# Scores of two heads into one double bank of PSUM, shared with the projections' sums

## The chip, the cores and the metric

The kernel runs on one core of a Trainium2 chip. The metric is device time in microseconds (us) of one execution. The engines are named as in the profile: PE (TensorE, matmuls; PEld its weight loads), DVE (VectorE), ACT (ScalarE), POOL (GpSimd), SP (SyncE, which issues the DMAs). PSUM, which the matmuls write, has eight banks of 512 fp32 numbers in each of 128 partitions; DVE and ACT read their sums from there.

## The reference

A stack of decoder layers on x of 256 positions by 1024, all in fp32: two layers of feed-forward, attention, feed-forward, and then a second block with other mixers and a routed feed-forward. The edit touches the attentions of the two first layers. NSA (16 query heads of 64, 4 key heads) adds a compressed branch, a selected one and a window one under gates; at 256 positions the last two have all keys in reach. DIFF (8 heads) takes the difference of two softmaxes per head:

```python
def dense_diff_attention(q, k, v, slopes, lmbda):
...
        sc = jnp.einsum('bhctd,bhcsd->bhcts', qi, k).astype(f32) * scale \
            - slopes[:, None, None, None] * dist
        p = masked_softmax(sc, dist >= 0)
        a = p[:, :, 0] - lmbda * p[:, :, 1]
        return jnp.einsum('bhts,bhsd->bhtd', a.astype(v.dtype), v)

def nsa_mixer(h, w_in, w_out, q_norm, k_norm, cmp_pos, cmp_w1, cmp_w2):
...
    o_cmp, o_sel = nsa_compressed_selected(q, kc, vc, ks, vs, slopes)
    o_win = banded_attention(q, kw, vw, slopes, NSA_WINDOW)
    g = jax.nn.sigmoid(gates.reshape(B, S, NSA_HKV, G, 3).transpose(0, 2, 3, 1, 4))
    o = g[..., 0:1] * o_cmp + g[..., 1:2] * o_sel + g[..., 2:3] * o_win
    return o.transpose(0, 3, 1, 2, 4).reshape(B, S, NSA_HQ * dh) @ w_out
...
        x = x + 0.5 * swiglu(rmsnorm(x, ffn1_norm[layer]), ffn1_w_in[layer], ffn1_w_out[layer])
...
        x = x + y
        x = x + 0.5 * swiglu(rmsnorm(x, ffn2_norm[layer]), ffn2_w_in[layer], ffn2_w_out[layer])
```

## The kernel before

x stays in SBUF as two tiles of 128 rows. Weights are streamed: SP loads a piece `raw`, ACT rounds it to `whi` (L123), DVE takes the rest `wlo` (L124), and a product with it is three matmuls (L183 to L185: high by high, low by high, high by low; 128x512 each). A projection chunk (`proj_chunk`, L277) sums both row tiles over 1024 inputs: 48 such matmuls into two banks, which `pair` (L194) hands out. `out_proj` (L303) sums the attention's output against its weights into four banks.

NSA runs its parts in an order written out by hand. "a" is an attend of row tile i and key head g, "q" the second query projection, "c" the compressed branch of a tile, "k" its combine, "m" the compression and "o" the output's parts:

```python
NSA_ORDER = "m a00 a01 a10 a11 q c0 a02 a03 o k0 c1 a12 a13 k1"
```

The first query projection, queries(0), stands ahead of all that. A query projection is the chunk, then for each tile an evacuation on ACT (L579), a square (L494), a sum and an inverse root on DVE (L495 on), a product (L581), four transposes on PE (L584) and a copy on ACT (L585). An attend (L664) computes, for each of four heads, a score matmul (L674) whose contraction has 64 rows, rows 0 to 63 for even heads and 64 to 127 for odd ones, and then two softmax parts: DVE adds the bias and takes the minimum in one pass (L504), ACT exponentiates (L507). Probabilities are scaled, transposed (L694), copied (L696, L698) and multiplied by v (L700). The compressed branch's first products are L714, the combine's L747.

DIFF projects six chunks in the order 2, 0, 4, then attends two row tiles of the first four heads, then 1, 3, 5 and the other four heads. An attend (L822) has two scores per head, again on rows 0 to 63 and 64 to 127 (L833), the two softmax parts, the difference, transposes (L843) and the product with v (L846). At the end the output is split and transposed (L233).

Within these lists the order on each engine is worked out by a scheduler when the kernel is built: what stands later in the program can be put between earlier instructions of an engine, where its banks and buffers are free. The banks are dealt out in pools. In NSA: tp two, mm two (projections, compression), sa two (scores), ot one, cm one. In DIFF: tp two, mm two, sa two, pa one, ot one. After the attends all but tp are closed, and the same six banks are dealt again, four of them as mm for `out_proj`.

## Time and profile before

| | us |
|---|---|
| three runs | 2269.57, 2267.53, 2270.04 |
| median | 2269.57 |
| the profiled execution, its own time | 2267.65 |
| its span in the profile | 2265.9 |
| PE busy | 2214.5 |
| DVE busy | 1643.8 |
| ACT busy | 1137.3 |

The span is the stretch from the first to the last recorded instruction of the profiled execution; its own time is 1.75 us longer. Busy times are sums over the records of an engine. A matmul's record is longer than the step from one to the next, since they are pipelined: a row of 0.39 us in a timeline follows the one before it by 0.23. NSA's attention lies between some 225 and 385 us of the span, DIFF's between 750 and 930.

### The profile page before, as it was taken

How to read it: one execution, taken by the hardware profiler on the slowest of the kernel's cores; microseconds unless marked ns; L12 is line 12 of the kernel's file. 1: busy time of each engine (PE TensorE's matmuls, PEld its weight loads, DVE VectorE, ACT ScalarE, POOL GpSimd, SP SyncE). 2: the span in 40 equal slices, each digit the busy share in tenths (PEclk: the TensorE clock that was granted, in tenths of full speed). 3: DMA queues.
4: the chain of work that ended last, by engine and by line, in shares of the span. 5: the costliest groups of instructions: out<-in, count | busy, mean ns of one | idle time of the engine just before them, and what ended most of it. 6: DMA issues, size and time to landing. Idle time of an engine off the chain costs nothing. (4 is left out here: it accounts for less than half of the span.)

```text
span 2265.9 us, 35790 instructions
## 1 busy us (share of the span) xinstructions
PE 2214.5 (98%) x13730; PEld 1875.1 (83%) x13730; DVE 1643.8 (73%) x3303; ACT 1137.3 (50%) x1789; POOL 33.3 (1%) x75
## 2 busy tenths in 40 slices
PE   8999999999999998999999999999999999999999
PEld 7887646888788776888787777999999998888887
DVE  6867666997787587787577567896767767885555
ACT  6554575554555464655455444454533344334443
POOL 1000000000000002000000000000000000000000
PEclk9999989999999997999999999999999999999999
DMA  6654424888655442555432125445544445445554
GB/s 215 195 190 170 154 70 148 298 272 269 237 198 182 166 150 74 163 190 193 130 138 85 66 85 194 140 168 195 184 161 149 150 167 186 159 155 180 195 194 150
DMA packets 107563, 383.33 MB, mean 169 GB/s; under 512 B 13440, under 2 KB 13824, under 8 KB 107392
## 3 DMA queue, kind: packets, MB, share of 16 engines
q1 hardware_dynamic: 103392, 374.39, 48.7%
q10 hardware_dynamic: 3360, 4.55, 0.6%
q8 instruction: 108, 1.77, 0.3%
q0 software_dynamic: 640, 2.11, 0.3%
q14 instruction: 63, 0.52, 0.1%
HBM read 378.89 MB, written 2.11 MB: 168 GB/s over the span
## 5 line engine op out<-in xcount | busy, mean ns | idle before, releaser
L123 ACT ACTIVATE whi<-raw 128x1024 fp32r<-128x1024 f32 x654 | 690.7, 1059 | 767.5 <-PE pout L184 205.0
L124 DVE TENSOR_TENSOR wlo<-raw,whi 128x1024 fp32r<-128x1024 f32 x654 | 797.7, 1223 | 327.1 <-ACT whi L123 318.7
L191 PE MATMUL pair<-xx,whi 128*128 128x512 f32 x1280 | 449.8, 396 | 0.0
L192 PE MATMUL pair<-xx,wlo 128*128 128x256 f32 x1280 | 359.8, 281 | 0.0
L183 PE MATMUL pu<-xx,whi 128*128 128x256 f32 x1024 | 292.6, 286 | 1.1 <-ACT H L1628 1.1
L184 PE MATMUL pu<-xx,wlo 128*128 128x256 f32 x1024 | 290.2, 283 | 0.0
L185 PE MATMUL pu<-xx,whi 128*128 128x256 f32 x1024 | 290.1, 283 | 0.0
L191 PEld LDWEIGHTS pair<-xx,whi 128*128 128x128 f32 x1280 | 240.8, 188 | 55.7 <-issue 0.2
L192 PEld LDWEIGHTS pair<-xx,wlo 128*128 128x128 f32 x1280 | 242.7, 190 | 0.5 <-issue 0.2
L183 PE MATMUL pout<-whi,hs 128*128 128x512 f32 x512 | 201.4, 394 | 0.2 <-ACT hs L1715 0.2
L184 PE MATMUL pout<-whi,hs 128*128 128x512 f32 x512 | 199.5, 390 | 0.2 <-DVE hs L1716 0.2
L185 PE MATMUL pout<-wlo,hs 128*128 128x512 f32 x512 | 199.6, 390 | 0.0
L183 PEld LDWEIGHTS pu<-xx,whi 128*128 128x128 f32 x1024 | 197.0, 192 | 1.3 <-ACT H L1628 1.3
L184 PEld LDWEIGHTS pu<-xx,wlo 128*128 128x128 f32 x1024 | 196.5, 192 | 0.0
L185 PEld LDWEIGHTS pu<-xx,whi 128*128 128x128 f32 x1024 | 196.4, 192 | 0.0
L183 PE MATMUL pair<-whi,hT 128*128 128x512 f32 x352 | 138.5, 393 | 6.6 <-DVE x L350 6.6
L185 PE MATMUL pair<-wlo,hT 128*128 128x512 f32 x352 | 139.2, 396 | 0.0
L184 PE MATMUL pair<-whi,lT 128*128 128x512 f32 x352 | 138.3, 393 | 0.0
L183 PE MATMUL bank<-whi,xx 128*128 128x512 f32 x288 | 118.0, 410 | 1.1 <-DVE rsg L167 0.5
L184 PE MATMUL bank<-whi,xx 128*128 128x512 f32 x288 | 115.7, 402 | 0.0
L185 PE MATMUL bank<-wlo,xx 128*128 128x512 f32 x288 | 114.9, 401 | 0.0
L185 PEld LDWEIGHTS pout<-wlo,hs 128*128 128x128 f32 x512 | 96.1, 188 | 20.2
(562 smaller groups left out, 3505.5 us busy)
## 6 DMA issues: line engine op xcount, KB each, us to landing
raw<-in_pu_dram SPq DMA_DIRECT2D x128, 512.0 KB, 3.5
raw<-in_pv_dram SPq DMA_DIRECT2D x128, 512.0 KB, 3.5
raw<-in_f1i_dram SPq DMA_DIRECT2D x88, 512.0 KB, 4.1
raw<-in_f2i_dram SPq DMA_DIRECT2D x88, 512.0 KB, 4.3
araw<-in_wada_dram SPq DMA_DIRECT2D x48, 512.0 KB, 4.7
raw<-in_f1o_dram SPq DMA_DIRECT2D x44, 512.0 KB, 3.5
raw<-in_f2o_dram SPq DMA_DIRECT2D x44, 512.0 KB, 3.7
raw<-in_wi_dram SPq DMA_DIRECT2D x28, 512.0 KB, 3.4
```

Source lines behind the costliest of these rows:

```text
L123: nc.scalar.activation(hi, raw, AF.Copy)
L124: nc.vector.tensor_tensor(lo, raw, hi.bitcast(F32), op=OP.subtract)
L183: mm(out, lh, rh, start=start, stop=False)
L184: mm(out, ll, rh, start=False, stop=False)
L185: mm(out, lh, rl, start=False, stop=stop)
L191: mm(out, lh, rr, start=start, stop=False)
L192: mm(out[:, 0], ll, rr[:, 0], start=False, stop=stop)
```

## The change

A pool of two double banks ("pairs") takes the place of mm and sa in both attentions. `pair` now hands out one double bank for a projection chunk, the compression takes half of one, and an attend takes one for the scores of two heads (NSA) or of a head's two softmaxes (DIFF). Both score matmuls are written ahead of the softmax parts of either. ot, cm and pa are opened ahead of the pairs. Bank counts stay eight.

```diff
+    def pair_banks(self, ctx, n):
+
+        self.mm = ctx.enter_context(self.tc.tile_pool(name=self.name("pairs"), bufs=n, space=PSUM, reuse_waits="tile"))
+        self.pairs = True
...
-            self.banks(first, mm=2, sa=2, ot=1, cm=1)
+            self.banks(first, ot=1, cm=1)
+            self.pair_banks(first, 2)
...
-                ph = self.bank(self.mm, 256)
+                ph = self.pair()[1][0][:, :256]
...
-                for j in range(4):
-                    h = 4 * g + j
-                    r = slice(64 * (h % 2), 64 * (h % 2) + 64)
-                    ps = self.bank(self.sa, 512)
-                    nc.tensor.matmul(ps[:, :n], qT[r, h // 2, t], KT[r, g, :n], start=True, stop=True)
-                    for b in range(2):
-                        src = ps[:, :n].rearrange("p (k c) -> p k c", c=256)[:, :, b * P:(b + 1) * P]
-                        self.softmax_part(src, self.bias[:, h, 1 - i:], i + 1, sums[:, b, j:j + 1], prob[j][:, b])
+                for j in range(0, 4, 2):
+
+                    ps = self.pair()[1]
+                    for e in range(2):
+                        r = slice(64 * e, 64 * e + 64)
+                        nc.tensor.matmul(ps[e][:, :n], qT[r, 2 * g + j // 2, t], KT[r, g, :n], start=True, stop=True)
+                    for e in range(2):
+                        for b in range(2):
+                            src = ps[e][:, :n].rearrange("p (k c) -> p k c", c=256)[:, :, b * P:(b + 1) * P]
+                            self.softmax_part(src, self.bias[:, 4 * g + j + e, 1 - i:], i + 1, sums[:, b, j + e:j + e + 1],
+                                              prob[j + e][:, b])
...
+            self.pairs = False
             first.close()
             self.banks(ctx, mm=4)
...
-            self.banks(first, mm=2, sa=2, pa=1, ot=1)
+            self.banks(first, pa=1, ot=1)
+            self.pair_banks(first, 2)
...
-                    prob = []
+                    prob, ps = [], self.pair()[1]
                     for e in range(2):
                         r = slice(64 * e, 64 * e + 64)
-                        ps = self.bank(self.sa, 512)
-                        nc.tensor.matmul(ps[:, :n], qT[r, h, t], kT[r, h, :n], start=True, stop=True)
-                        prob.append(self.softmax_part(ps[:, :n].rearrange("p (k c) -> p k c", c=P),
+                        nc.tensor.matmul(ps[e][:, :n], qT[r, h, t], kT[r, h, :n], start=True, stop=True)
+                    for e in range(2):
+                        prob.append(self.softmax_part(ps[e][:, :n].rearrange("p (k c) -> p k c", c=P),
                                                       self.bias[:, 2 * h + 1, 1 - i:], i + 1, rsum[:, e:e + 1]))
...
+            self.pairs = False
             first.close()
             self.banks(ctx, mm=4)
```

The order on PE, which waits for one instruction after the other, changes in four places; three are shown. Line numbers of the change are some units higher: scores are L680 (NSA) and L842 (DIFF), the transposes of the queries L589, of the probabilities L702 and L853, the products L708 and L856, c0's first L722, the combine L755.

In NSA, PE beside attends a10 and a11. Before, matmuls of the second query projection (those into bank_3010 and bank_3011) stand between the scores:

```order
L674 MATMUL bank_2825<-KT,qT 128x512
L184 MATMUL bank_3011<-whi_2560,xx_1855 128x512
L185 MATMUL bank_3011<-wlo_2561,xx_1855 128x512
L183 MATMUL bank_3010<-whi_2574,xx_1855 128x512
L639 MATMUL bank_2616<-cw_1847,h_2528 15x64 x16
L674 MATMUL bank_2835<-KT,qT 128x512
L694 MATMUL bank_2801<-ident,prob_2744 128x128
L694 MATMUL bank_2801<-ident,prob_2745 128x128
```

After, in the same place, there are none:

```order
L708 MATMUL bank_2714<-pT_2725,v 64x256 x2
L680 MATMUL pair_2814<-KT,qT 128x512 x2
L644 MATMUL bank_2609<-cw_1844,h_2521 15x64 x16
L680 MATMUL pair_2833<-KT,qT 128x512 x2
L702 MATMUL bank_2790<-ident,prob_2735 128x128
```

Its 48 matmuls (now into pair_2995) begin later, 18 of them beside the end of a11, and the last 30 follow a11's last product in one piece. This is where that piece ends: the transposes of the new queries (L589), then c0 (L722) and the next scores stand directly behind it.

```order
L183 MATMUL pair_2995<-whi_2573,xx_1852 128x512
L184 MATMUL pair_2995<-whi_2573,xx_1852 128x512
L185 MATMUL pair_2995<-wlo_2574,xx_1852 128x512
L589 MATMUL bank_3089<-ident,q_3068 128x128 x4
L589 MATMUL bank_3116<-ident,q_3095 128x128 x4
L722 MATMUL bank_3123<-qT,KT 32x256 x2
L680 MATMUL pair_3160<-KT,qT 128x256 x2
```

Before, the tail of a11 stood between the projection's last matmul and those transposes.

At NSA's end, PE beside the last attend (a13, L700, L694) before: the output projection (into bank_3604 and 3605) starts while a13 still has transposes and products to do, 15 matmuls ahead of the last combine.

```order
L700 MATMUL bank_3440<-pT_3460,v 64x256
L700 MATMUL bank_3440<-pT_3469,v 64x256 x2
L183 MATMUL bank_3604<-whi_2594,oh_3325 128x512
L184 MATMUL bank_3604<-whi_2594,oh_3325 128x512
L185 MATMUL bank_3604<-wlo_2595,oh_3325 128x512
L183 MATMUL bank_3605<-whi_2594,oh_3325 128x512
L184 MATMUL bank_3605<-whi_2594,oh_3325 128x512
L185 MATMUL bank_3605<-wlo_2595,oh_3325 128x512
L183 MATMUL bank_3604<-whi_2600,oh_3325 128x512
```

After, its first matmul (into bank_3579) stands behind the last product of the attend and the last combine (L755):

```order
L708 MATMUL bank_3511<-pT_3531,v 64x256 x2
L755 MATMUL bank_3549<-cpT_2519,vb 64x128
L708 MATMUL bank_3511<-pT_3540,v 64x256 x2
L755 MATMUL bank_3549<-cpT_2519,vb 64x128 x7
L755 MATMUL bank_3561<-cpT_2519,vb 64x128 x8
L183 MATMUL bank_3579<-whi_2587,oh_3305 128x512
L184 MATMUL bank_3579<-whi_2587,oh_3305 128x512
L185 MATMUL bank_3579<-wlo_2588,oh_3305 128x512
```

At DIFF's end the same happens: 23 output matmuls stood beside the last attend and its transposes, and after the change the first stands behind the last of these (L238).

In DIFF's first half, PE beside the first two attends before: projection matmuls (into bank_8018 and 8019, a chunk of the other heads) stand between the scores, 24 up to the last score.

```order
L833 MATMUL bank_7780<-dkT,dqT 128x128
L833 MATMUL bank_7787<-dkT,dqT 128x128
L183 MATMUL bank_8018<-whi_7626,xx_7336 128x512
L184 MATMUL bank_8018<-whi_7626,xx_7336 128x512
L833 MATMUL bank_7804<-dkT,dqT 128x128
L833 MATMUL bank_7811<-dkT,dqT 128x128
L185 MATMUL bank_8018<-wlo_7627,xx_7336 128x512
L183 MATMUL bank_8018<-whi_7626,xx_7336 128x512
L184 MATMUL bank_8018<-whi_7626,xx_7336 128x512
L185 MATMUL bank_8018<-wlo_7627,xx_7336 128x512
L183 MATMUL bank_8019<-whi_7626,xx_7336 128x512
L833 MATMUL bank_7828<-dkT,dqT 128x128
```

After, the scores of the first attend follow each other, and no projection matmul stands ahead of the last score (row by row it goes on with scores, L853 and L856 only):

```order
L185 MATMUL pair_7672<-wlo_7579,xx_7308 128x512
L842 MATMUL pair_7749<-dkT,dqT 128x128 x2
L842 MATMUL pair_7772<-dkT,dqT 128x128 x2
L842 MATMUL pair_7795<-dkT,dqT 128x128 x2
L842 MATMUL pair_7818<-dkT,dqT 128x128 x2
L842 MATMUL pair_7861<-dkT,dqT 128x256
L853 MATMUL bank_7766<-ident,pr_7760 128x128
L842 MATMUL pair_7861<-dkT,dqT 128x256
L856 MATMUL bank_7747<-dv,pT_7767 128x128
```

## Rows read from the trace of the kernel before

**Rows 1.** The profile page: the span; then busy time, share of the span and number of instructions of each engine; then the granted TensorE clock in 40 equal slices of the span, in tenths (9 is 90% or more).
```profile
span 2265.9 us, 35790 instructions
...
PE 2214.5 (98%) x13730; PEld 1875.1 (83%) x13730; DVE 1643.8 (73%) x3303; ACT 1137.3 (50%) x1789; POOL 33.3 (1%) x75
...
PEclk9999989999999997999999999999999999999999
```

**Rows 2.** A table by stretch (start and end in us, length; busy time of PE, weight loads, DVE, ACT and POOL with the number of instructions; granted clock; DMA share; GB/s). The first line is NSA's attends up to where c0 goes on, the second c0 and the later attends up to the first matmul of the output projection, the third the end of the last NSA attend and the combine; the fourth and the fifth are the first two attends of DIFF's first half and of its second half.
```profile
274.23:318.40 44.17, 41.74 (x213) 22.59 (x213) 35.43 (x124) 35.11 (x90) 0.00 (x0) 0.96 0.43 144
318.40:360.14 41.74, 38.98 (x172) 18.21 (x172) 22.30 (x109) 25.03 (x89) 0.00 (x0) 0.71 0.02 6
360.14:369.96 9.82, 9.80 (x81) 6.91 (x80) 3.53 (x10) 4.57 (x13) 1.02 (x2) 1.00 0.37 140
820.40:838.00 17.60, 17.51 (x76) 10.64 (x76) 12.32 (x59) 13.23 (x39) 0.00 (x0) 1.00 0.26 91
869.87:886.16 16.29, 15.99 (x50) 8.54 (x49) 10.53 (x54) 8.98 (x33) 0.00 (x0) 0.67 0.18 63
```

**Rows 3.** The timeline of PE around NSA's first query projection: its last matmul, and the transposes of its two tiles of 128 rows. Columns, here and in every timeline below: start in us, length of the row, engine, line, operation, output <- inputs, shapes, count, and in brackets the idle time just before and what ended it.
```profile
256.07 0.39 PE L185 MATMUL bank<-wlo,xx 128*128 128x512 f32 x1
...
260.97 0.66 PE L584 MATMUL bank<-ident,q 128*128 128x128 f32 x4
...
262.33 0.66 PE L584 MATMUL bank<-ident,q 128*128 128x128 f32 x4
```

**Rows 4.** The timeline of DVE in the same place: the first reduction of the normalisation of the queries, and the last product, that of the second tile.
```profile
256.52 0.69 DVE L495 TENSOR_REDUCE ss<-sq 128x8 f32<-128x512 f32 x1 [7.37 <-ACT sq L494]
...
261.39 0.69 DVE L581 TENSOR_TENSOR q<-q,rsy 128x512 f32<-128x512 f32 x1
```

**Rows 5.** Groups of instructions by line and shape, 264 to 370 us (total busy us, mean ns of one | idle time before them): the split of a weight piece, and the copy of the transposed queries, the evacuation of the projection and its square.
```profile
L123 ACT ACTIVATE whi<-raw 128x1024 fp32r<-128x1024 f32 x10 | 10.5, 1051 | 1.5 <-PE bank L184 1.5
...
L585 ACT ACTIVATE qT<-bank,gq 128x512 f32<-128x512 f32 x2 | 1.4, 677 | 0.1
L579 ACT ACTIVATE q<-bank,rsy 128x512 f32<-128x512 f32 x2 | 1.3, 674 | 0.7 <-PE bank L185 0.7
...
L494 ACT ACTIVATE sq<-q 128x512 f32<-128x512 f32 x2 | 1.3, 630 | 0.1
```

**Rows 6.** The timeline of PE around the end of NSA's second query projection: its last matmul, transposes of a11's probabilities, a11's last product, and the first matmul of c0 that needs the new queries.
```profile
308.10 0.40 PE L185 MATMUL bank<-wlo,xx 128*128 128x512 f32 x1
...
309.32 1.13 PE L694 MATMUL bank<-ident,prob 128*128 128x128 f32 x8 [0.27 <-DVE prob L687]
...
316.49 0.65 PE L700 MATMUL bank<-pT,v 128*64 128x256 f32 x4
...
318.40 0.62 PE L714 MATMUL bank<-qT,KT 64*32 64x256 f32 x4 [0.78 <-ACT qT L585]
```

**Rows 7.** The timeline of PE at NSA's end: the first matmul of the output projection, and the one with which it goes on after the combine.
```profile
360.14 0.50 PE L183 MATMUL bank<-whi,oh 128*128 128x512 f32 x1
...
369.96 0.50 PE L183 MATMUL bank<-whi,oh 128*128 128x512 f32 x1
```

**Rows 8.** The timeline of PE in DIFF's first half: two projection matmuls nine steps apart, the first scores of the attends, a later score alone, and the last score.
```profile
818.04 0.39 PE L185 MATMUL bank<-wlo,xx 128*128 128x512 f32 x1
...
820.08 0.39 PE L185 MATMUL bank<-wlo,xx 128*128 128x512 f32 x1
820.40 0.49 PE L833 MATMUL bank<-dkT,dqT 64*128 64x128 f32 x4
...
827.62 0.70 PE L833 MATMUL bank<-dkT,dqT 64*128 64x256 f32 x2
...
836.21 0.70 PE L833 MATMUL bank<-dkT,dqT 64*128 64x256 f32 x2
```

**Rows 9.** The timeline of PE in DIFF's second half: the first scores, a score alone, the last score of these two attends, and the first matmul of the output projection.
```profile
869.87 0.49 PE L833 MATMUL bank<-dkT,dqT 64*128 64x128 f32 x4
...
875.66 1.22 PE L833 MATMUL bank<-dkT,dqT 64*128 64x256 f32 x2
...
886.16 1.22 PE L833 MATMUL bank<-dkT,dqT 64*128 64x256 f32 x2
...
894.14 0.77 PE L183 MATMUL bank<-whi,doh 128*128 128x512 f32 x1
```

**Rows 10.** The timeline of PE in NSA's first attends: two scores next to each other (four instruction records), and one score by itself (two records).
```profile
265.21 0.70 PE L674 MATMUL bank<-KT,qT 64*128 64x256 f32 x4
...
270.26 0.70 PE L674 MATMUL bank<-KT,qT 64*128 64x256 f32 x2
```

**Rows 11.** A table by stretch, columns as in rows 2: c0 and its followers in NSA, in two parts, and DIFF's second half in two parts.
```profile
315.81:326.01 10.20, 8.36 (x49) 3.88 (x48) 5.62 (x35) 7.89 (x30) 0.00 (x0) 1.00 0.00 1
326.01:349.90 23.89, 22.87 (x88) 10.73 (x92) 9.22 (x47) 12.27 (x45) 0.00 (x0) 0.50 0.00 1
...
869.87:875.60 5.73, 5.43 (x27) 3.40 (x26) 4.90 (x29) 4.74 (x17) 0.00 (x0) 0.99 0.50 178
875.60:896.00 20.40, 17.20 (x46) 9.94 (x45) 10.57 (x52) 7.59 (x27) 6.04 (x5) 0.50 0.00 0
```

**Rows 12.** The waits of DVE between 318.4 and 368 us, by the instruction that waited and what it waited for (us in total, times, longest).
```profile
DVE sc L504 <- PE bank L674: 12.8, 6, 4.3
```

**Rows 13.** The timeline of PE in DIFF's projections: a matmul that waited for its bank.
```profile
797.55 0.50 PE L183 MATMUL bank<-whi,xx 128*128 128x512 f32 x1 [0.51 <-ACT qk L811]
```

More of the change, by code (lines that the diff above doesn't have):

```diff
@@ L360, in ffn @@
             self.banks(ctx, tp=2)
-            self.mm = ctx.enter_context(tc.tile_pool(name=self.name("pairs"), bufs=3, space=PSUM, reuse_waits="tile"))
-            self.pairs = True
+            self.pair_banks(ctx, 3)
             hT = ht.tile([P, 22, S], F32R, name=self.name("hT"), tag="hT")
```

## The prediction

> **What bounds the kernel now.** I read the page's shares first: PE is busy 98% of the span and DVE 73%, at a granted clock near full [rows 1]. So the default is that time is made of PE's work, and that a change counts by what it does to gaps on PE, to PE's own work, or to its clock. Then I took the two attention stages, the only places the edit touches, stretch by stretch [rows 2]. The reader is to see that PE is covered nearly everywhere, also beside the attends, although an attend is a chain through DVE and ACT. That is because other matmuls stand between an attend's own: in NSA the second query projection beside attends a10 and a11, then the first matmuls of the output projection beside the last attend; in DIFF the value projection and, at the end, the output projection. One such 128x512 matmul costs 0.227 us at full clock: nine steps from 818.04 to 820.08 [rows 8]. Third, the clock: where no such matmuls stand between, the granted clock falls to about half, 1.2 GHz in place of 2.4 [rows 11]. DIFF's second pair of attends begins at 869.87 with nothing but its own matmuls and transposes; to 875.60 the clock is 0.99, from there to 896 it is 0.50, and one score of 256 columns goes from 0.70 to 1.22 us [rows 8, 9].
>
> So the question is not how long a score takes, but which matmuls stand between the attends' after the change. That is a matter of banks: until now projections and scores had two banks each of their own, and a projection's chunk could be summed while scores came and went. Now a chunk holds one of two double banks from its first matmul to its last reader, in the program's order with the scores.
>
> **The change part by part.** The sum is made against the profiled execution, 2267.65 us (span 2265.9). The median of the runs, 2269.57, is 1.9 us above it; 0.2% of it, 4.5 us, is about what a measurement of this kernel can tell from no change.
>
> (A) The chain behind NSA's second query projection. Before, its last matmul is at 308.10 and the tail of a11 (309.32 to 317.1) covers the chain from it to the transposes; c0 goes on at 318.40 with a wait of only 0.78 [rows 6]. After, the last 30 of the 48 matmuls stand in one piece behind a11's last product, and nothing stands between them and the transposes. The length of that chain is taken from the means of its parts and from the first query projection, which does the same work. On ACT: one split still ahead of it (1.05), two evacuations (0.67 each) and a square (0.63), 3.0 together [rows 5]. On DVE: from the first reduction at 256.52 [rows 4] to the transposes at 260.97 and 262.33 [rows 3], 4.5 and 5.8. Then the transposes (0.66) and the copy on ACT (0.68). The second tile, which c0 stands behind on PE, is done 3.0 + 5.8 + 0.7 = 9.5 behind the projection's end. When is that end? Thirty matmuls, 6.8 us, move from beside the attends to behind them. Had the stretch been bound by PE, the attends would end 6.8 earlier and the projection at 317.1 as they did; had they gained nothing, at 323.9. DVE is busy 35.43 and ACT 35.11 of 44.17 [rows 2], so there is room to shorten, and I take 6 of the 6.8: the projection ends at 317.9, c0 starts at 327.4 in place of 318.40: +9. Bounds: +4, if the attends shorten by all of DVE's slack (8.7), no split is in the way and c0 needs only the first tile (0.67 + 0.63 + 4.5 + 0.66 + 0.68 = 7.1): 317.1 − 8.7 + 6.8 + 7.1 = 322.3; +15 if the attends gain nothing.
>
> (B) NSA's end. The output projection takes four banks. Before, they were those of mm and sa, free early, and 15 of its matmuls run from 360.14 on beside the last attend and the combine; the rest follow at 369.96 [rows 7]. After, they are the banks of ot, cm and one pair, and its first matmul stands behind the last combine. 15 x 0.227 = 3.4 of cover gone. If that stretch gets as much shorter, nothing is lost, but DVE is busy 3.53 and ACT 4.57 of its 9.82 [rows 2], so it is a chain of short steps that doesn't shrink with PE's work: +3, bounds 0 and 3.4.
>
> (C) DIFF's first two attends. 24 projection matmuls (5.5 us) stand between their scores before, none up to the last score after. Their price can be read: from first to last score, 820.40 to 836.21, 15.8 with the fillers [rows 8], and 869.87 to 886.16, 16.3 without, the clock having dropped [rows 9]. The same time, and 5.5 of work to be done later: +5, bounds 0 and 5.5.
>
> (D) DIFF's end. 23 output matmuls stand beside the last attend (from 894.14 on [rows 9]), none after: 5.2. Part of them only waited for the transposes behind them: +4, bounds 0 and 5.2.
>
> (E) The clock outside these stretches. After an unfilled stretch the dense matmuls begin at half clock. NSA's c0 and its followers now run at full from 315.81 to 326.01 and at half for the 24 us behind it [rows 11]; behind a hole of 9.5 us I expect half from the start. The 8.36 us that PE is busy in those first 10.20 would about double where PE bounds, and half that where it does not; a few of the first output matmuls add 0.2 each. I take +5, bounds 0 and +12.
>
> (F) The gain. Two scores on rows 0–63 and 64–127, next to each other, take the time of one: 0.70 for two at 265.21, 0.70 for one alone at 270.26 [rows 10]. But many already were neighbours. By the order on PE, adjacency is won for three NSA pairs of 512 columns (1.05 each) and five DIFF pairs of 128 (0.42), and lost for one pair of 256 in either stage (0.63): 3.2 + 2.1 − 1.3 = 4.0. Double-buffered projection chunks remove bank waits like the 0.51 at 797.55 [rows 13]. I take −3, since where DVE and ACT bound the attend PE's saving is idle time; bounds −8 and −1. In the Trainium skill, the page "TensorEngine Tiling (Array Packing)", section Performance Considerations, PSUM Bottleneck, says that packing speeds up TensorE but not the reading of PSUM, which may become the limit. By it (F) would be worth nothing and the sum 3 us more; DVE's waits for scores, above, say that in part of NSA it is still TensorE that DVE waits for.
>
> Here is that row: between 318.40 and 368 DVE waits 12.8 us for scores, six times [rows 12]. There the clock is half and one score of 512 columns takes 2 us. Emitting both at once helps only where the second was late for want of its own issue.
>
> The other edits (the helper, compress' sum in a pair) only change a name or take one more bank for a short time; pricing them at nothing assumes that the other pair is free then, which the next projection needs only after a11's scores.
>
> Sum: 9 + 3 + 5 + 4 + 5 − 3 = +23, so 2267.65 + 23 = 2290.7, say 2291.
>
> **The rivals.**
> Faster: DVE's 12.8 us of waits for scores vanish [rows 12] and lead the whole stage, while the displaced matmuls cost nothing because each stretch shrinks by them (B to E are zero). Then 9 − 12.8 − 3 = −7: 2261. It speaks for it that those waits are the largest in NSA; against it that PE is then at half clock, so that the score is late because PE is slow, not because it was issued late. It decides if B to E come to under 7 while all 12.8 go.
> No change: PE really bounds every stretch (it is busy 9.80 of 9.82 in NSA's end [rows 2]), so matmuls moved out shorten it by as much; B to E zero, A at its lower bound, F −3: 2269. Against it is the pair of DIFF stretches under (C).
> Much slower: the clock stays down through all of NSA's later attends and into both output projections, and a10 and a11 don't shorten: A 13, E 12, F −2: 13 + 3 + 5 + 4 + 12 − 2 = +35, 2303.
>
> **How the numbers follow.** Forecast (2280 to 2298) 0.58; much slower 0.22; no change, or up to 2280, 0.12; faster 0.08. The predicted time is the likeliest, 2291. The range leaves out most of the faster case and the part of the slow one above its bounds: 2274 to 2308, the low end being the sum with A at 4, B and D at 0, C at 3, E at 2 and F at −3 (2274). Of the no-change case I give half to "same": same 0.06, faster 0.08, slower 0.86.
>
> **What would show it.** (A): a gap on PE of 6 to 10 us between the last matmul of the second query projection and its transposes, released through ACT's copy. (B) and (D): the first output matmul starts only after the last combine or transpose, and PE shows waits for DVE and ACT in the last attend. (C): the first score to the last in some 16 us at a clock well under 1. (E): half clock from c0 on. (F): score pairs as one block of 0.70. I am wrong if the attends a00 to a11 shorten by more than the moved matmuls, if the gap in (A) is under 4, or if the clock stays full in the unfilled attends.

## The result and the profile after

The change made the kernel slower: 2293.87 us median (2291.17 to 2294.75, 4 runs) against 2268.55 for the kernel before in the runs beside it; ratio 1.0121, 95% interval 1.0099 to 1.0144. The forecast was 2291 with a range of 2274 to 2308. The profiled execution took 2293.91 us with a span of 2291.7, 25.8 more than before.

The page of the changed kernel: span, busy times, and the granted clock in 40 slices.

```profile
span 2291.7 us, 35797 instructions
...
PE 2213.2 (97%) x13730; PEld 1879.7 (82%) x13730; DVE 1644.8 (72%) x3303; ACT 1137.9 (50%) x1789; POOL 33.2 (1%) x75
...
PEclk9999979999999987899999999999999999999999
```

PE's busy time is the same (2213 us, 2214 before [rows 1]) in a longer span, so in these two traces the 26 us appear as time in which PE waits. What the clock costs lies inside the busy time and can't be read from this: the mean granted clock is 0.974 here and 0.984 before. Where the lag grows is read by taking the same event in both timelines of PE:

| event | before | after | lag |
|---|---|---|---|
| last matmul of NSA's second query projection | 308.10 | 317.12 | +9.0 |
| c0's first matmul behind the query transposes | 318.40 | 326.77 | +8.4 |
| last row of combine matmuls in NSA | 368.11 | 372.43 | +4.3 |
| last output matmul of NSA | 389.17 | 396.90 | +7.7 |
| last output matmul of the feed-forward ahead of DIFF | 782.48 | 793.25 | +10.8 |
| first DIFF score | 820.40 | 830.69 | +10.3 |
| last score of DIFF's first two attends | 836.21 | 845.26 | +9.1 |
| first score of DIFF's second half | 869.87 | 888.17 | +18.3 |
| last score of DIFF's second half | 886.16 | 904.99 | +18.8 |
| last output matmul of DIFF | 926.50 | 953.52 | +27.0 |

Each trace is of one execution, and the kernel before took between 2252.33 and 2277.98 us in the runs beside the experiments. In the run below that changes DIFF alone, NSA is the code of before and its last output matmul stands at 386.84 in place of 389.17. So a step of two or three us between two traces is not settled by them.

The gap behind the second query projection, timeline of PE after (it answers to [rows 6]):

```profile
317.12 0.39 PE L185 MATMUL pair<-wlo,xx 128*128 128x512 f32 x1
324.34 1.09 PE L589 MATMUL bank<-ident,q 128*128 128x128 f32 x4 [6.83 <-DVE rsy L173]
325.75 1.09 PE L589 MATMUL bank<-ident,q 128*128 128x128 f32 x4 [0.32 <-DVE q L586]
326.77 1.07 PE L722 MATMUL bank<-qT,KT 64*32 64x256 f32 x4
```

PE stands 6.83 us between the projection's last matmul and the first transposes, where a11's tail stood before. NSA's end, after (it answers to [rows 7]):

```profile
372.43 1.96 PE L755 MATMUL bank<-cpT,vb 128*64 128x128 f32 x30
374.31 0.50 PE L183 MATMUL bank<-whi,oh 128*128 128x512 f32 x1
```

No output matmul starts ahead of the last combine; 15 did before. And DIFF's second two attends, PE and then DVE, after (they answer to [rows 9]):

```profile
892.84 1.22 PE L842 MATMUL pair<-dkT,dqT 64*128 64x256 f32 x2
893.99 0.79 PE L856 MATMUL bank<-dv,pT 128*128 128x128 f32 x2
894.71 1.22 PE L842 MATMUL pair<-dkT,dqT 64*128 64x256 f32 x2
...
896.26 1.22 PE L842 MATMUL pair<-dkT,dqT 64*128 64x256 f32 x2
...
898.14 1.22 PE L842 MATMUL pair<-dkT,dqT 64*128 64x256 f32 x2
```

```profile
895.97 0.42 DVE L508 CUSTOM_DVE_ANT_0 sc<-pair,bias 128x256 f32<-128x256 f32 x1 [1.65 <-PE pair L842]
...
897.14 0.40 DVE L508 CUSTOM_DVE_ANT_0 sc<-pair,bias 128x256 f32<-128x256 f32 x1
...
899.39 0.42 DVE L508 CUSTOM_DVE_ANT_0 sc<-pair,bias 128x256 f32<-128x256 f32 x1 [1.52 <-PE pair L842]
...
902.82 0.42 DVE L508 CUSTOM_DVE_ANT_0 sc<-pair,bias 128x256 f32<-128x256 f32 x1 [1.29 <-PE pair L842]
```

These rows hold what I had not seen. A double bank holds the scores of a head's two softmaxes here. The first score runs from 892.84 for 1.22 us and is done at 894.06; the second stands behind a product (L856) and runs from 894.71 to 895.93. DVE reads the first score at 895.97, when the second is done, and the second at 897.14. The next pair repeats it (898.14 plus 1.22 is 899.36; DVE's next read 899.39). So the softmax part of the first score waits for both scores of the double bank. In the kernel before it waits for its own alone: the score of 877.54 ends at 878.76 and is read at 878.80.

```profile
877.54 1.22 PE L833 MATMUL bank<-dkT,dqT 64*128 64x256 f32 x2
...
880.97 1.22 PE L833 MATMUL bank<-dkT,dqT 64*128 64x256 f32 x2
```

```profile
878.80 0.42 DVE L504 CUSTOM_DVE_ANT_0 sc<-bank,bias 128x256 f32<-128x256 f32 x1 [1.12 <-PE bank L833]
```

What this wait costs is another question. The table by stretch, from behind the drop of the clock to the last score, in the kernel before and in the change (columns as in [rows 2]), and DVE's waits for scores in these two attends of the kernel before:

```profile
875.66:886.16 10.50, 10.50 (x24) 5.15 (x23) 5.57 (x26) 4.25 (x16) 0.00 (x0) 0.50 0.00 1
```

```profile
892.44:904.99 12.55, 12.55 (x28) 6.21 (x26) 6.07 (x34) 4.67 (x20) 0.00 (x0) 0.50 0.02 9
```

```profile
DVE sc L504 <- PE bank L833: 4.2, 4, 1.7
```

PE has no gap in either and runs at a granted clock of 0.50, the lower of its two levels; a head takes it 3.4 us in both (892.84 to 896.26, and 877.54 to 880.97). DVE waits 4.2 us for scores before and, as is shown below, 5.1 in the change. In these rows it is PE at the lower clock that sets the pace, with single banks as with pairs, and DVE's waits go along with it.

### The profile page after: what moved, and what is told of

Read it like the earlier page. It is cut to its first block, busy times and chain, and to the rows that moved or that the text cites. A ratio compares the mean times of both kernels' runs of the same rounds, so it can differ in the third digit from the quotient of the medians.

```text
span 2291.7 us, 35797 instructions
## 1 busy us (share of the span) xinstructions
PE 2213.2 (97%) x13730; PEld 1879.7 (82%) x13730; DVE 1644.8 (72%) x3303; ACT 1137.9 (50%) x1789; POOL 33.2 (1%) x75
## 4 chain that ended last, share of the span: by engine, by line
PE 83%; DVE 9%; ACT 3%; DMA 3%; issue 1%; POOL 1%; SPq 0%; ACTq 0%; DVEq 0%
PE pair L191 13%; PE pair L192 6%; PE pout L183 5%; PE pout L184 5%; PE pout L185 5%; PE pu L183 5%; PE pu L184 5%; PE pu L185 5%; PE pair L183 4%; PE pair L184 4%; PE pair L185 4%; DVE wlo L124 3%; PE pw L1681 3%; PE bank L183 3%; PE bank L184 2%; PE bank L185 2%
## 5 line engine op out<-in xcount | busy, mean ns | idle before, releaser
L184 PEld LDWEIGHTS pout<-whi,hs 128*128 128x128 f32 x512 | 96.2, 188 | 19.9 <-DVE hs L1727 0.6
L183 PEld LDWEIGHTS pout<-whi,hs 128*128 128x128 f32 x512 | 96.5, 189 | 19.4 <-ACT hs L1726 0.3
L183 PE MATMUL pair<-whi,xx 128*128 128x512 f32 x240 | 96.9, 404 | 3.1 <-DVE x L355 3.1
```

Source lines behind the costliest of these rows:

```text
L183: mm(out, lh, rh, start=start, stop=False)
L184: mm(out, ll, rh, start=False, stop=False)
```

## Experiments

Three theories went into the first four runs: the loss is cover that went with the sharing of banks (1), it is the pairing itself (2), it is the clock (3). A second question came with the rows above: if pairing costs, is it because DVE's first read waits for the second score (P), because a double bank comes free only as a whole (R), or because the clock falls (C)? All ratios are to the kernel before, in runs beside it.

**Pairs with a double bank of their own.** `pair_banks(first, 1)` for the projections, and a second pool of one double bank for the scores, both opened ahead of the others:

```diff
-            self.banks(first, ot=1, cm=1)
-            self.pair_banks(first, 2)
+            self.pair_banks(first, 1)
+            self.banks(first, sa=1)
+            self.banks(first, ot=1, cm=1)
...
-                    ps = self.pair()[1]
+                    ps = self.score_pair()
```

(`score_pair` hands out the double bank of `sa`; DIFF likewise.)

> Scores still go in pairs into one double bank, but a double bank of their own (one), and the projections have the other (one); both are opened ahead of ot, cm and pa. By the order on PE, 42 projection matmuls stand between DIFF's first scores again, 31 output matmuls beside DIFF's last attend, 12 beside NSA's, and 52 attend matmuls between the second query projection and its transposes. Theory 1 (the loss is cover that went because projections and scores draw from the same double banks and because the output projection's banks come free late): 2262 to 2274 us, the gap of 6.8 us before the query transposes gone. Theory 2 (the loss is the pairing: a double bank comes free only when both heads are read): at least 2290, since the scores have half as many double banks as in the change. Theory 3 (most of the loss is the half clock of score pairs without pauses): 2280 to 2290.

Measured: 2293.99 us, ratio 1.0121 (1.0099 to 1.0143), as slow as the change. Theory 1 fell as the whole story: the cover is all there and the time is not. The waits of DVE (270 to 400 us) and of PE (225 to 400) in NSA in this run, by who waited for what (us in total, times, longest):

```profile
DVE sc L513 <- PE spair L686: 25.2, 9, 6.5
```

```profile
PE spair L686 <- DVE nm L513: 7.4, 4, 2.4
```

DVE waits 25.2 us for scores, and PE 7.4 for the one double bank to be read. With one double bank a new pair can't begin until both heads are read; that is R, where there is just one. In this trace 24 of the 32 pairs stand next to each other on PE, 17 in the change, so it is not by more parted pairs that this run is slow.

**Shared single banks, opened late.** No pairs: four single banks for projections and scores, behind ot and cm (pa and ot):

```diff
-            self.banks(first, mm=2, sa=2, ot=1, cm=1)
+            self.banks(first, ot=1, cm=1, mm=4)
...
-                    ps = self.bank(self.sa, 512)
+                    ps = self.bank(self.mm, 512)
```

> Four single banks shared by projections and scores, opened behind ot, cm and pa as in the change; scores are written one by one as before, with no pairs. Theory 1: the cover is gone just as in the change (no projection matmul between DIFF's first scores, no output matmul beside the last attends, two matmuls between the query projection and its transposes), and what pairing gains is missing: 2290 to 2300 us. Theory 2: 2265 to 2272, since nothing is paired. Theory 3: between, about 2280.

Measured: 2273.73 us, 1.0049 (1.0028 to 1.0069): not before's time and not the change's.

**The pairs opened first.** The change with the two lines that open the pools exchanged, in NSA and in DIFF:

```diff
-            self.banks(first, ot=1, cm=1)
-            self.pair_banks(first, 2)
+            self.pair_banks(first, 2)
+            self.banks(first, ot=1, cm=1)
```

> The change with one thing undone: the pairs are opened ahead of ot, cm and pa, so that the output projection's four banks are those of the two pairs and come free with the last scores. 13 output matmuls stand beside NSA's last attend again and 23 beside DIFF's; the gap behind the second query projection and DIFF's first attends stay as in the change. Theory 1: DIFF's end gives back some 7 to 8 us (its lag grew from 18.8 to 27.0 between the last score and the last output matmul), NSA's end 0 to 3: 2282 to 2288 us. Theory 2: as the change, 2290 to 2296.

Measured: 2281.20 us, 1.0073 (1.0052 to 1.0093). In the profile the lag between DIFF's last score and its last output matmul grows by 1.6 us (13.8 to 15.4) where it grew by 8.2 in the change. That part of theory 1 holds.

**Shared single banks, opened first.**

```diff
-            self.banks(first, mm=2, sa=2, ot=1, cm=1)
+            self.banks(first, mm=4, ot=1, cm=1)
```

> The four shared single banks of the run above, opened ahead of ot, cm and pa: 15 and 21 output matmuls stand beside the last attends again. Theory 1: 7 to 11 us below the run above, 2281 to 2290 us, and 0 to 4 above the pairs opened first. Theory 2: 2265 to 2272.

Measured: 2260.12 us, 0.9989 (0.9970 to 1.0008): theory 1 expected 2281 to 2290 and was wrong by 20 us; theory 2 (2265 to 2272) came nearer. Sharing costs nothing here, though the projection matmuls are gone from between the scores just as in the change, and though PE still waits 4.8 us behind the second query projection. What it wins in return is seen in DIFF's second attends. PE, the table by stretch of this run from first to last score:

```profile
869.04:877.00 7.96, 7.96 (x42) 4.93 (x41) 6.97 (x42) 6.80 (x26) 0.00 (x0) 1.00 0.43 128
```

Before, the same stretch took 16.3 us at a clock of 0.67 [rows 2]; here 7.96 at full clock. PE is busy for 7.96 of 7.96 us here and for 15.99 of 16.29 before, so the two differ in the clock and not in PE's waits. DVE waits once for a score here, 1.7 us. The changed kernel, by contrast, from first to last score:

```profile
888.17:904.99 16.82, 15.30 (x47) 7.97 (x46) 9.16 (x50) 8.59 (x32) 0.00 (x0) 0.59 0.15 57
```

This goes through the whole study: in the six runs with four single banks or with all of DIFF's pairs adjacent, the granted clock in DIFF's second attends is 1.00; in the eight other kernels it is 0.59 to 0.70. Why it holds in the six is not shown.

One thing has to be allowed for. In this run, in the one opened late and in the two below with single banks, the edit also caught line 1427: a third attention, in the block behind, takes its scores from mm in place of sa. From DIFF's last output matmul to the end of the span these four profiles take 1334.7 to 1335.8 us, the ten others of this study 1336.1 to 1342.1 with a median of 1338.1. So some 3 us (0.0014 of the ratio) of their time belong to that line. Without them the ratios would be 1.0063 (late) and 1.0003 (first); this is worked out, not run.

**All pairs adjacent.** The pairs opened first, and the score matmuls with a higher priority in the scheduler:

```diff
                         r = slice(64 * e, 64 * e + 64)
-                        nc.tensor.matmul(ps[e][:, :n], qT[r, h, t], kT[r, h, :n], start=True, stop=True)
+                        with tc.high_priority(200):
+                            nc.tensor.matmul(ps[e][:, :n], qT[r, h, t], kT[r, h, :n], start=True, stop=True)
```

> The pairs opened first, and the two score matmuls of a pair given a higher priority in the scheduler, so that all 32 pairs stand next to each other on PE (16 and 0 of DIFF's, 5 and 4 of NSA's were neighbours as counted by rows of the order; now all). Theory P (the pairs lose because DVE's first read of a double bank waits for the second head's score, which stood behind other matmuls on PE): the waits of DVE for scores in DIFF's second attends fall from 5.1 us to under 2, those attends take some 8 to 11 us in place of 16.8, and the time is 2258 to 2270 us. Theory R (they lose because a double bank comes free only when both heads are read, so fewer scores are in flight): adjacency helps little, 2276 to 2283. Theory C (it is the clock: score pairs leave PE idle so that it falls to half): the same as R unless the granted clock rises.

(The count of neighbours in DIFF should read 8 pairs, not 16.) Measured: 2265.93 us, 1.0016 (0.9998 to 1.0034), 0.0057 or 13 us below the same pools without the priority. The table by stretch and DVE's waits for scores in DIFF's second attends:

```profile
868.74:878.45 9.71, 7.95 (x50) 4.94 (x50) 7.83 (x42) 7.63 (x27) 0.00 (x0) 1.00 0.35 113
```

```profile
DVE sc L508 <- PE pair L844: 0.9, 1, 0.9
```

The same waits in the changed kernel:

```profile
DVE sc L508 <- PE pair L842: 5.1, 4, 1.7
```

The stretch takes 9.7 us in place of 16.8, the waits 0.9 in place of 5.1. So what pairs cost goes when their two matmuls stand next to each other; that is clear of noise. Through what it goes is not shown. Theory P foretold this, but C, too, allowed for it if the clock rises, and it rose from 0.59 to 1.00 in the stretch. The pages of the pairs opened first and of this run:

```profile
span 2279.8 us, 35794 instructions
PE 2209.1 (97%) x13730; PEld 1876.3 (82%) x13730; DVE 1645.4 (72%) x3303; ACT 1136.3 (50%) x1789; POOL 33.3 (1%) x75
```

```profile
span 2259.6 us, 35803 instructions
PE 2182.3 (97%) x13730; PEld 1861.3 (82%) x13730; DVE 1645.7 (73%) x3303; ACT 1135.1 (50%) x1789; POOL 33.4 (1%) x75
```

With the pairs adjacent PE is busy 26.8 us less for as many matmuls, and idle for 77.3 us in place of 70.7 (a wait of 8.5 us at DIFF's end, which the last runs take up, is among them). So what the span wins here is not PE's waits: its matmuls take less time, at a median granted clock of 0.985 over the runs in place of 0.980. (This trace is the fastest of its twelve runs, 4 us below their median.) Whether parted pairs bring the clock down through DVE's waits or in another way is open, and the priority moved other instructions too (six projection matmuls stand in each of DIFF's attend groups). Against single banks opened first this run is 0.0013 slower by the corrected ratio, inside the interval: being in pairs neither costs nor gains once they are adjacent. A cost of R is not to be seen in the time with two double banks, though the change has waits of its kind (PE waits 1.8 us for the readers of dv and 1.5 for those of scores in DIFF's first half).

**NSA alone, and DIFF alone.** Each is the change with the other attention's lines as they were, as here for DIFF (in the second run the same for NSA):

```diff
-            self.banks(first, pa=1, ot=1)
-            self.pair_banks(first, 2)
+            self.banks(first, mm=2, sa=2, pa=1, ot=1)
...
-                    prob, ps = [], self.pair()[1]
+                    prob = []
```

> The change in NSA alone; DIFF as before. By the lag of the changed kernel's trace behind the one before (7.7 us at NSA's last output matmul, 10.8 at the start of DIFF, 25.8 at the end) NSA's part, with the half clock behind it in the feed-forward, is 8 to 11 us: 2272 to 2276. The prediction's terms for NSA (A 9, B 3, E 5, and some 2 of the gain) gave 15: 2279.

> The change in DIFF alone; NSA as before. By the same lags 15 to 16 us: 2279 to 2281. The prediction's terms for DIFF (C 5, D 4, less 1 of the gain) gave 8: 2272.

Measured: NSA alone 2279.59, 1.0071 (1.0044 to 1.0097); DIFF alone 2285.26, 1.0084 (1.0058 to 1.0111). In the profiles the lag at DIFF's last output matmul is 11.3 and 15.7, together the change's 27.0. The medians add up to 0.0155 where the change has 0.0121; the three intervals allow that, so how the loss divides is known to some 5 us only. NSA's share by its median (16) is nearer the prediction's 15 than the trace's 11.

**The second query projection earlier, in the change.**

```diff
-NSA_ORDER = "m a00 a01 a10 a11 q c0 a02 a03 o k0 c1 a12 a13 k1"
+NSA_ORDER = "m a00 a01 q a10 a11 c0 a02 a03 o k0 c1 a12 a13 k1"
```

> The change with one thing moved: NSA's second query projection is written two attends earlier, between a01 and a10, so that 10 attend matmuls stand between its end and its transposes in place of none. If the gap of 6.8 us there is the price that (A) names, it falls under 2 us and the time to 2285 to 2289. If the attends only shift, because the projection takes a double bank from the scores wherever it stands, 2291 to 2296.

Measured: 2289.18 us, 1.0101 (1.0068 to 1.0133). The wait of PE there, in the change and in this run:

```profile
PE bank L589 <- DVE rsy L173: 6.8, 1, 6.8
```

```profile
PE bank L589 <- DVE q L586: 1.1, 1, 1.1
```

The gap went from 6.8 to 1.1 us, the median fell by 4.7 and the lag at NSA's last output matmul by 1.5 (7.7 to 6.3). The intervals overlap, so the fall is not established; by the lag, most of what the gap held moved elsewhere.

**The same with single banks, opened first.** The same order, in the kernel of four shared banks.

> The four shared single banks opened first (no pairs), with NSA's second query projection written two attends earlier, between a01 and a10; 13 attend matmuls then stand between the projection's end and its transposes in place of 2. If the gap of 5.7 us there is the price of sharing that (A) names, it shrinks to under 2 and the time falls by 3 to 6 us against the same kernel with the projection in its old place, to 2254 to 2258. If the chain behind the projection is hidden in another way or the attends just move, it stays at 2258 to 2262.

Measured: 2258.67 us, 0.9983 (0.9957 to 1.0009), 1.4 us below the same without the new order. Inconclusive, and it agrees with the run above: the gap itself is worth little.

**Masks on POOL.** In the run with shared banks opened first, what the faster attends win is partly lost at DIFF's end. PE and DVE there:

```profile
882.72 0.46 PE L843 MATMUL bank<-ident,pr 128*128 128x128 f32 x2 [1.27 <-DVE pr L839]
891.83 1.12 PE L233 MATMUL bank<-ident,do 128*128 128x128 f32 x4 [8.65 <-DVE do L853]
```

```profile
884.15 0.14 DVE L170 TENSOR_TENSOR rst<-rsy 128x4 f32<-128x4 f32 x1
887.58 0.87 DVE L981 COPY lmask<-lm 64x64 f32<-64x64 f32 x1 [3.28 <-POOL lm L954]
...
891.08 0.69 DVE L853 TENSOR_TENSOR do<-bank,rsy 128x512 f32<-128x512 f32 x1
```

DVE is to normalise DIFF's first output (L853), but ahead of it in its queue stand copies of a constant mask for the next block, which wait for POOL; PE waits 8.65 us for that. The next three runs put those fills and copies on POOL, in the kernel before, in the shared single banks and in the adjacent pairs, the last two with the earlier query projection:

```diff
-                nc.vector.memset(w, -1.0)
+                nc.gpsimd.memset(w, -1.0)
...
-                    nc.vector.tensor_copy(self.lmask[r, lv], w[r, r])
+                    nc.gpsimd.tensor_copy(self.lmask[r, lv], w[r, r])
```

> The kernel before, with the constant masks of the block behind DIFF (L973, L981) filled and copied by POOL in place of DVE. In the shared-banks run DVE waits 3.3 us for POOL between the parts of DIFF's last normalisation and PE idles 8.7 us behind it; before, DVE's waits there are 5.6 us in all. If that wait is what takes back the gain of faster attends, here 2 to 5 us go: 2259 to 2262. If PE's work at DIFF's end covers it before, the same as before, 2262 to 2266.

> Four shared single banks opened first, no pairs, the second query projection two attends earlier, and the masks on POOL. If the wait on the masks takes back the attends' gain, PE's 8.7 us of idle time in DIFF's end fall under 3 and the time to 2249 to 2254, below the kernel before beyond its interval. If not, as without the masks' move, 2257 to 2261.

> The same with pairs: two double banks opened first, all score pairs adjacent by priority, the query projection earlier, the masks on POOL. Theory P says that adjacent pairs lose nothing for being pairs, but their next pair waits for both heads' reads: 0 to 6 us above the run with single banks, 2251 to 2259. If pairs side by side also save time on PE that matters, it is below it, 2245 to 2249.

Measured: before with masks on POOL 2262.98, 0.9988 (0.9965 to 1.0010), no difference; shared single banks 2252.39, 0.9951 (0.9925 to 0.9977); adjacent pairs 2256.56, 0.9960 (0.9942 to 0.9978). PE's waits for L853 in DIFF's second half, shared single banks without and with the masks on POOL:

```profile
PE bank L233 <- DVE do L853: 8.8, 2, 8.7
```

```profile
PE bank L233 <- DVE do L853: 2.1, 2, 1.8
```

Both beat the kernel before, clear of noise; with the 3 us of line 1427 taken off, the single banks come to 0.9965, level with the pairs. That the masks matter only beside faster attends is not shown, though. DVE waits for POOL in the kernel before as well, and with the masks on POOL its stretch from the first score of DIFF's second half to the last output matmul falls from 56.6 us (869.87 to 926.50) to 49.8:

```profile
DVE lmask L981 <- POOL lm L954: 5.6, 4, 4.0
```

```profile
872.34 0.49 PE L833 MATMUL bank<-dkT,dqT 64*128 64x128 f32 x4
...
922.16 0.39 PE L185 MATMUL bank<-wlo,doh 128*128 128x512 f32 x1
```

In the single banks with the early projection the same step is from 52.2 to 44.7, about as much. The intervals of the three runs with masks on POOL overlap, so how much of the gain over the kernel before belongs to the masks, and how much to the attends, is open.

## Why the prediction was right, point by point

The time, the sign and the two places were right, and the gap, the lost cover and the clock are all to be seen. But the price of sharing was set too high and that of pairing too low, even with the wrong sign; the two errors cancel in the sum. That 2291 came within 3 us of 2293.87 is therefore in part luck: it is added up from terms that are not what the time is made of.

**What the sum missed.** By the ratios, sharing of banks costs nothing (1.0003 corrected), opening them late 0.0060 without pairs and 0.0048 with them (13.6 and 10.9 us of 2265), and pairing, with the matmuls of many pairs parted, 0.0058 late and 0.0070 first (13 and 16 us, corrected). Each of these is a difference of two ratios and known to some 0.003, 7 us. Late banks and parted pairs together make the change's 0.0121. The first of them I had, in (B) and (D), with 7 us; the second I had not.

**(A), the gap: there, but hardly the loss.** 6.83 us between the projection and its transposes, c0 late by 8.4 where I said 9. But closing it gave back 1.5 us of lag, and 4.7 of the median, which is not clear of noise. I priced the gap as if PE's idle time there were all lost; with the gap closed, the rest of NSA took longer, and with four single banks a gap of 4.8 us goes with no loss at all.

**(B), NSA's end: right in kind, size not settled.** From the last combine to the last output matmul the lag grows from 4.3 to 7.7, the 3.4 us of 15 matmuls that now come behind. Whether the attends ahead got shorter by as much, the change alone doesn't tell. With the pairs opened first the lag falls by 6.5 from the last row of query transposes to the last output matmul (10.8 to 4.3) where it rises by 1.6 in the change (6.2 to 7.7). But the pairs opened first had come to those transposes 4.6 us later; at NSA's last output matmul the two traces are 3.4 us apart, no more than the matmuls.

**(C), DIFF's first attends: the matmuls right, the reason wrong.** The lag grows by 8.0 from the first score to the first score of the second half; I had 5. Moved work is 24 matmuls, 5.4 us. The rest is PE's waits for a double bank to be read (1.8 and 1.5 us), and matmuls at half clock behind the attends. But the step "the same time with and without fillers" was read from a stretch [rows 9] whose pace was set by PE at half clock. With four single banks the clock stays up and the stretch takes 8.0. The sharing that took the cover away would have paid for it.

**(D), DIFF's end: right in kind, half the size.** 8.2 in place of 4: all 23 matmuls (5.2) and 3 us more; PE there now waits 3.7 us for L863 (L853 before), where matmuls stood before.

**(E), the clock: there, its size not settled.** From c0 on the clock was half from the start, as I expected: the transposes ahead of it take 1.09 us a row in place of 0.66. Yet c0's stretch, which I had in this term, was no slower than before; the lag falls from 8.4 to 4.3 up to the combine. Between NSA's end and DIFF the lag grows by 3.0 us, where PE goes on at half clock behind a short gap. The timeline of PE at the end of the feed-forward behind NSA, in the kernel before, in the change, and in the kernel before with masks on POOL:

```profile
586.12 0.50 PE L183 MATMUL pair<-whi,hT 128*128 128x512 f32 x1 [2.60 <-DVE x L350]
586.46 0.39 PE L184 MATMUL pair<-whi,lT 128*128 128x512 f32 x1
```

```profile
594.42 0.80 PE L183 MATMUL pair<-whi,hT 128*128 128x512 f32 x1 [2.81 <-DVE x L355]
595.01 0.63 PE L184 MATMUL pair<-whi,lT 128*128 128x512 f32 x1
```

```profile
581.19 0.80 PE L183 MATMUL pair<-whi,hT 128*128 128x512 f32 x1 [2.45 <-DVE x L350]
581.78 0.63 PE L184 MATMUL pair<-whi,lT 128*128 128x512 f32 x1
```

The first two gaps are alike, 2.60 and 2.81 us, but after the second the matmul takes 0.80 us and the next follows 0.59 behind, in place of 0.50 and 0.34. The third shows the same half clock behind a gap of 2.45 us in a kernel with NSA as before. So this is not shown to come from the change: from NSA's last output matmul to the feed-forward's last, the kernel before takes 393.3 us, the change 396.4, and the adjacent pairs with masks on POOL, faster than either, 400.5.

**(F), the gain: wrong, and the sign too.** I took −3 from adjacent pairs and never asked what becomes of a pair whose two matmuls the scheduler parts. Side by side, pairs are worth nothing: all adjacent they are level with single banks (1.0016 against a corrected 1.0003). Apart, they cost 13 to 16 us. The rule weighed there, of the Trainium skill's page "TensorEngine Tiling (Array Packing)" (Performance Considerations, PSUM Bottleneck), that packing speeds up TensorE but not the reading of PSUM, was the better guide to the gain; it doesn't speak of the wait.

**The rivals.** The faster one rested on DVE's waits for scores in NSA [rows 12], 12.8 us. It was not empty: single banks or adjacent pairs, opened first, do shorten the attends. But the time does not show it (0.9989 and 1.0016). And it missed what the change does: PE's order parts the pair, so the waits stay (in DIFF's second attends 4.2 us before, 5.1 after).

## What to carry to other kernels

Where two results go into one buffer, a reader of the first can wait for the writer of the second: look, in the order on the engine, whether the two stand next to each other, and if not, make them or keep two buffers. Here that was worth 13 us or more, though not shown to come from the wait itself. When pools are opened again for a later stage, see which of the old buffers the next stage will get, and open the old pools so that these are the ones that come free first; the place of one line in either attention was worth 11 to 14 us here. And take the pace of a stretch from one with the buffers that the change will have, not from one that only lacks the same fillers, and look at the clock on both sides before you give the difference to a wait.

## What the runs showed that was not expected

DIFF's second attends ran 7.96 us at a granted clock of 1.00 with nothing but their own matmuls and transposes, when scores were seldom late; in the change they ran 16.8 us at 0.59, with PE at the lower of its two levels, 1.2 GHz, for most of it. I had read the half clock of [rows 11] as the mark of attends without other matmuls between. Which way cause runs is open. Half clock makes scores late; but late scores did not leave PE idle once the clock had fallen (12.55 of 12.55 us busy). Nor does idle time just ahead of the fall explain it by itself: up to the fall PE was busy 2.02 of 3.17 us in the change and 5.43 of 5.73 before [rows 11], while with adjacent pairs it was busy 5.13 of the first 6.25 us and the clock stayed at 1.00. No run held the one fixed.
